# A four-stage transformer stack on one core: the instruction order of every engine chosen with another timing model

## The chip, the cores and the metric

The kernel runs on one core of one Trainium2 chip. The time is the device time of one execution in microseconds (us). The core's engines work side by side, each through its own list of instructions in a fixed order: TensorE (PE) multiplies matrices, VectorE (DVE) and ScalarE (ACT) do elementwise work, GpSimd (POOL) a little of it, and SyncE (SP) issues the transfers from memory. An instruction that has to wait holds up all that stand behind it on its engine. PE adds up its products in PSUM, a small memory from which DVE and ACT read them; everything else lies in SBUF.

## The reference

A sequence of 512 tokens of width 1024 goes through two blocks, all in float32. Only the shape of the work matters here:

```python
def first_block(x, mem, ...):
    h = token_mixer(rmsnorm(x, norm_mix_pre), ...)          # four kinds of token mixing, then @ w_mix_out
    x = x + rmsnorm(h, norm_mix_post)
    h = memory_cross_attention(rmsnorm(x, norm_cross_pre), rmsnorm(mem, mem_norm), wq, wk, wv, wo)
    x = x + rmsnorm(h, norm_cross_post)
    h = conv_glu_ffn(rmsnorm(x, norm_ffn_pre), w_up, conv_w, conv_b, w_down)
    x = x + rmsnorm(h, norm_ffn_post)
    return x

def second_block(x, ...):
    x = x + _even_mixer(x, ...)        # window attention and neighbourhood attention
    x = x + _mlp(x, norm, w1, w2)      # square(relu(h @ w1)) @ w2, hidden width 4096
    x = x + _odd_mixer(x, ...)         # retention with gates
    x = x + _mlp(x, norm, w1, w2)
    return x
```

What matters below are the three lines `x = x + rmsnorm(h, gain)` of the first block. The norm of a whole product `h` has to be known before anything of the next stage can start.

## The kernel before

The activations lie transposed: a row of the model width on each partition, the 512 tokens along the free axis, so the residual stream is eight tiles `X0` to `X7` of 128x512. Each float32 product is made of three faster ones. Both factors are split into a rounded high part and a low part (the rest), and `mm3` issues high by high (L272), high by low (L273) and low by high (L274). An activation is split by ACT (L280, high part, with the gain of the norm as scale) and DVE (L281, low part). A weight tile arrives by a transfer as `wf`, ACT casts it into `wh` (L315) and DVE takes the difference into `wl` (L316). There are four buffers for `wf`, six for `wh` and six for `wl`. A cast for a seventh tile therefore waits until PE has used the one six tiles back.

At the very start the norm of `x` is computed from eight squares (ACT) and sums (DVE L415), one product with a matrix of ones on PE (L420, `total`), then `rsqrt`: two ACT instructions (L295, L296) and three DVE instructions (L297 to L299). DVE L755 multiplies `X` by the result, and L280 and L281 split the product into the tiles `x` that the mixer's weights are multiplied with. While this runs, PE works on products with `mem`, for the cross attention.

The end of each of the mixer, the cross attention and the feed-forward part is written in `out_post`. I call the three places the boundaries. The tokens are worked on in two halves of 256, A and B:

1. The last output tiles are computed for half A, squared (ACT L414), summed (L415) and scaled by the gain (ACT L614). `norm(A)` then is L420 on PE, L295 and L296 on ACT, and L297 to L299 on DVE.
2. While PE computes half B of the last tiles, `update(A)` works through the eight tiles of the residual stream. For each there are four instructions: DVE L622 (times the norm), DVE L623 (add to `X`), ACT L280 and DVE L281 (split for the next stage's weights).
3. PE multiplies half A of the new `x` with three weight tiles of the next stage, 72 products of 128x256. The same is then done with half B, its squares being summed by POOL (L415) ahead of its norm. The squares of the new `X` (ACT L629, sums L631 and L633 on POOL or DVE) serve the norm of the next stage.

```python
def update(c, ms=range(NK)):
    for m in ms:
        x = self.X[m][:, c]
        nc.vector.tensor_tensor(hg[m][:, c], hg[m][:, c], r[:, c], op=ALU.mult)
        nc.vector.tensor_tensor(x, x, hg[m][:, c], op=ALU.add)
        self.split(xs[0][m][:, c], xs[1][m][:, c], x, scale=self.vec(nxt, m))
```

The order in which instructions stand on each engine isn't that of the program text. All is written inside a `TileContext`, which collects the instructions, their dependences and the buffers they need, and at its end lists them anew. It walks through time with a model of how long each instruction takes. Whenever an engine is free in the model, it appends the earliest instruction of the text whose inputs and buffers the model then takes to be ready. What the model thinks of durations and waits so decides which instruction comes first where several could. The order so found is fixed. On the chip each engine follows it, with semaphores for the dependences.

After the third boundary come the even mixer (to about 1060 us in the profiled execution), and then the first MLP, the odd mixer and the second MLP.

## Time and profile before

| | |
|---|---|
| time, median of 3 runs | 2175.26 us (2174.89 to 2177.64) |
| the profiled execution | 2179.55 us |
| its span (first to last instruction) | 2177.8 us |
| PE busy / weight loads / DVE / ACT / POOL | 98% / 83% / 72% / 53% / 2% |
| places where the stages end (boundaries) | 333 to 367, 404 to 444 and 786 to 821 us |

The profile is of one execution of the program. Each row gives instructions by the line of the kernel that issued them, their start and duration, and, where the engine stood idle before, for how long and what ended the wait. The profiled execution was 4.3 us longer than the median of the runs, and 1.75 us of it lie outside the span.

### The profile page before, as it was taken

The page shows a single profiled execution, that of the slowest core. Times are in us where ns is not written, and L with a number is a line of the kernel's source. Part 1 is how long each engine was busy: PE and PEld are TensorE (multiplying, and loading weights), DVE is VectorE, ACT ScalarE, POOL GpSimd, SP SyncE. Part 2 cuts the span into 40 slices and gives each one's busy share as a digit, 9 for nine tenths or more (in the row PEclk, how much of TensorE's full clock was granted, in tenths as well). Part 3 has the DMA queues.
Part 4 walks back from the last instruction along what each step waited for, and adds up shares of the span by engine and source line. Part 5 has one row for each costly group of instructions (what it writes and reads, how often), then busy time and mean ns, then how long its engine had stood idle before and what let it go on. Part 6 is the DMA issues. An engine that isn't in the chain of part 4 may idle for free.

```text
span 2177.8 us, 31728 instructions
## 1 busy us (share of the span) xinstructions
PE 2140.9 (98%) x11942; PEld 1813.0 (83%) x11942; DVE 1571.4 (72%) x2852; ACT 1153.9 (53%) x2124; POOL 34.5 (2%) x54
## 2 busy tenths in 40 slices
PE   8999998899999999999999999999999999999999
PEld 7877788788888897777889889888888888898997
DVE  8867758787774268887977586756776579875864
ACT  6555656665554246677645344555555456543542
POOL 0000001100000010000000000000000000000000
PEclk9999999999999999999999999999999999999999
DMA  5211241132233322221432331322222223323322
GB/s 172 70 64 63 77 142 59 49 102 95 95 96 91 92 71 93 66 73 39 141 101 94 97 107 59 104 88 73 69 72 88 68 95 129 107 96 97 105 72 68
DMA packets 94762, 192.68 MB, mean 88 GB/s; under 512 B 10512, under 2 KB 12176, under 8 KB 94608
## 3 DMA queue, kind: packets, MB, share of 16 engines
q1 hardware_dynamic: 93744, 189.01, 27.1%
q8 instruction: 93, 1.52, 0.3%
q10 hardware_dynamic: 864, 1.64, 0.2%
q14 instruction: 61, 0.50, 0.1%
HBM read 188.52 MB, written 2.10 MB: 88 GB/s over the span
## 4 chain that ended last, share of the span: by engine, by line
PE 89%; DVE 6%; ACT 2%; DMA 2%; issue 1%; SPq 0%; DVEq 0%; ACTq 0%
PE acc L272 19%; PE acc L273 19%; PE acc L274 19%; PE sc L272 6%; PE sc L273 5%; PE sc L274 5%; PE pt L274 2%; PE pt L272 2%; PE pt L273 2%; PE o L272 2%; PE o L274 2%; PE o L273 2%; PE pt L510 1%; PE sc L910 1%; PE pt L420 1%; DVE wl L316 1%
## 5 line engine op out<-in xcount | busy, mean ns | idle before, releaser
L315 ACT CAST wh<-wf 128x512 fp32r<-128x512 f32 (+1 forms) x548 | 334.1, 616 | 537.1 <-PE acc L273 429.6
L316 DVE TENSOR_TENSOR wl<-wf,wh 128x512 fp32r<-128x512 f32 (+1 forms) x548 | 368.5, 682 | 184.4 <-ACT wh L315 172.3
L272 PE MATMUL acc<-x,wh 128*128 128x512 f32 (+1 forms) x1104 | 427.7, 389 | 5.1 <-ACT x L280 3.2
L273 PE MATMUL acc<-x,wh 128*128 128x512 f32 (+1 forms) x1104 | 427.4, 388 | 1.2 <-DVE x L281 1.1
L274 PE MATMUL acc<-x,wl 128*128 128x512 f32 (+1 forms) x1104 | 426.1, 387 | 0.0
L272 PEld LDWEIGHTS acc<-x,wh 128*128 128x128 f32 x1104 | 209.9, 191 | 51.2 <-issue 3.7
L273 PEld LDWEIGHTS acc<-x,wh 128*128 128x128 f32 x1104 | 210.1, 190 | 45.5 <-issue 2.9
L274 PEld LDWEIGHTS acc<-x,wl 128*128 128x128 f32 x1104 | 210.2, 190 | 44.3 <-issue 2.2
L286 ACT CAST Wh<-F 128x1792 fp32r<-128x1792 f32 x64 | 108.2, 1693 | 101.0 <-PE pt L273 63.2
L287 DVE TENSOR_TENSOR Wl<-F,Wh 128x1792 fp32r<-128x1792 f32 x64 | 129.2, 2020 | 30.5 <-ACT Wh L286 30.1
L274 PE MATMUL acc<-y,wl 128*128 128x512 f32 x288 | 113.7, 395 | 0.0
L273 PE MATMUL acc<-y,wh 128*128 128x512 f32 x288 | 113.6, 395 | 0.0
L272 PE MATMUL acc<-y,wh 128*128 128x512 f32 x288 | 113.3, 393 | 0.0
L273 PE MATMUL sc<-x,wh 128*128 128x512 f32 (+1 forms) x264 | 97.9, 373 | 5.3 <-DVE x L281 5.2
L272 PE MATMUL acc<-wh,x 128*128 128x256 f32 (+1 forms) x352 | 98.8, 281 | 0.0
L274 PE MATMUL acc<-wh,x 128*128 128x256 f32 (+1 forms) x352 | 98.8, 281 | 0.0
L273 PE MATMUL acc<-wl,x 128*128 128x256 f32 (+1 forms) x352 | 98.8, 281 | 0.0
L274 PE MATMUL sc<-x,wl 128*128 128x512 f32 (+1 forms) x264 | 97.3, 370 | 1.3 <-DVE wl L316 1.3
L272 PE MATMUL sc<-x,wh 128*128 128x512 f32 (+1 forms) x264 | 96.7, 372 | 1.5 <-ACT x L280 1.1
L272 PE MATMUL acc<-h,wh 128*128 128x512 f32 (+1 forms) x220 | 74.2, 337 | 0.0
L274 PE MATMUL acc<-h,wl 128*128 128x512 f32 (+1 forms) x220 | 74.1, 337 | 0.0
L273 PE MATMUL acc<-h,wh 128*128 128x512 f32 (+1 forms) x220 | 74.1, 337 | 0.0
(517 smaller groups left out, 5162.1 us busy)
## 6 DMA issues: line engine op xcount, KB each, us to landing
F<-in_w_mlp_in_dram SPq DMA_DIRECT2D x64, 512.0 KB, 3.2
wf<-in_w_mlp_out_dram SPq DMA_DIRECT2D x128, 256.0 KB, 2.8
wf<-in_w_ffn_in_dram SPq DMA_DIRECT2D x88, 256.0 KB, 2.7
wf<-in_w_o_fm_dram SPq DMA_DIRECT2D x64, 256.0 KB, 2.7
wf<-in_w_in_fm_dram SPq DMA_DIRECT2D x44, 256.0 KB, 2.9
wf<-in_w_ffn_out_dram SPq DMA_DIRECT2D x40, 256.0 KB, 2.7
wf<-in_w_o_v_dram SPq DMA_DIRECT2D x32, 256.0 KB, 3.0
wf<-in_w_out_o_dram SPq DMA_DIRECT2D x32, 256.0 KB, 2.8
```

The costliest lines, as they stand in the source:

```text
L272: mm(ps, lhsT=lh, rhs=rh, start=start, stop=False, skip_group_check=True)
L273: mm(ps, lhsT=lh, rhs=rl, start=False, stop=False, skip_group_check=True)
L274: self.last_mm = mm(ps, lhsT=ll, rhs=rh, start=False, stop=stop, skip_group_check=True).ins
L286: nc.scalar.copy(hi, src)
L287: nc.vector.tensor_tensor(lo, src, self.f(hi), op=ALU.subtract)
L315: nc.scalar.copy(h[:, :n], wf[:, :n])
L316: nc.vector.tensor_tensor(l[:, :n], wf[:, :n], self.f(h[:, :n]), op=ALU.subtract)
L420: self.nc.tensor.matmul(ps[:, :n], lhsT=self.ones if mat is None else mat, rhs=acc[:, :n], start=True, stop=True)
L510: nc.tensor.transpose(pt[:, c:c + 128], P[:, at:at + 128], self.ident)
L910: mm = lambda out, pr, ss, ts: nc.tensor.matmul(out, lhsT=kq[0][pr, ss], rhs=kq[1][pr, ts], start=True, stop=True, skip_group_check=True)
```

## The change

The timing model that the `TileContext` orders instructions by is the timeline simulation instead of the default one. The instructions, the buffers and the dependences are the same; only their order on each engine differs.

```diff
--- before.py
+++ after.py
@@ -1745,7 +1745,7 @@
     out = nc.dram_tensor("out_0_dram", (D, T), F32, kind="ExternalOutput").ap()
-    with tile.TileContext(nc) as tc:
+    with tile.TileContext(nc, schedule_with_timeline_sim=True) as tc:
         build(tc, A, out)
```

Three places show what moved. In the rows `pt` is a norm's total, `s_6724` the half's norm at the third boundary, `s_6726` to `s_6733` the eight scaled tiles, `X_70` to `X_77` the residual stream, and `x_7795`, `x_7796` the high and low part of the first new tile.

PE, first norm at the start of the program, before:

```order
L272 MATMUL acc_107<-qk_95,wh_170 128x512
L273 MATMUL acc_107<-m_103,wh_170 128x512
L420 MATMUL pt_237<-s_106,ones 128x512
L274 MATMUL acc_107<-qk_95,wl_171 128x512
L272 MATMUL acc_108<-qk_95,wh_191 128x512
```

and now:

```order
L273 MATMUL acc_109<-m_103,wh_212 128x512
L274 MATMUL acc_109<-qk_95,wl_213 128x512
L272 MATMUL acc_109<-qk_96,wh_212 128x512
L420 MATMUL pt_237<-s_106,ones 128x512
L273 MATMUL acc_109<-m_104,wh_212 128x512
L274 MATMUL acc_109<-qk_96,wl_213 128x512
L274 MATMUL acc_108<-qk_97,wl_192 128x512
L272 MATMUL acc_109<-qk_97,wh_212 128x512
L273 MATMUL acc_109<-m_105,wh_212 128x512
L274 MATMUL acc_109<-qk_97,wl_213 128x512
L272 MATMUL sc_382<-wh_360,x_275 128x256
L273 MATMUL sc_382<-wl_361,x_275 128x256
```

The total (L420) stood 48th on PE and now stands 67th, so 19 products of 128x512 have come ahead of it. Between it and the first product that needs the norm (`sc_382`, 74th in both) six products are left.

ACT at the third boundary, before:

```order
L295 ACTIVATE s_6724<-pt_7715,eps 128x256
L296 ACTIVATE s_6724<-s_6724 128x256
L315 CAST wh_7817<-wf_7815 128x512
L315 CAST wh_7823<-wf_7821 128x512
L315 CAST wh_7829<-wf_7827 128x512
L280 ACTIVATE x_7795<-X_70,vecs 128x256
L629 ACTIVATE s_6726<-X_70 128x256
L280 ACTIVATE x_7797<-X_71,vecs 128x256
```

and now:

```order
L315 CAST wh_7817<-wf_7815 128x512
L315 CAST wh_7823<-wf_7821 128x512
L315 CAST wh_7829<-wf_7827 128x512
L295 ACTIVATE s_6724<-pt_7715,eps 128x256
L296 ACTIVATE s_6724<-s_6724 128x256
L315 CAST wh_7835<-wf_7833 128x512
L315 CAST wh_7841<-wf_7839 128x512
L414 ACTIVATE s_7875<-acc_7269 128x256
```

Three weight casts have moved ahead of the two ACT steps of `norm(A)`; on DVE their three L316 stand ahead of L297 to L299 in the same way. The first boundary has the same move with three casts. At the second one cast now stands ahead of L295 and one between L295 and L296, and the four L316 of its casts stand ahead of and between L297 to L299.

DVE at the third boundary from the end of `norm(A)` on, before:

```order
L299 SCALAR_TENSOR_TENSOR s_6724<-s_7717,s_6724 128x256
L622 TENSOR_TENSOR s_6726<-s_6726,s_6724 128x256
L622 TENSOR_TENSOR s_6727<-s_6727,s_6724 128x256
L316 TENSOR_TENSOR wl_7818<-wf_7815,wh_7817 128x512
L316 TENSOR_TENSOR wl_7824<-wf_7821,wh_7823 128x512
L316 TENSOR_TENSOR wl_7830<-wf_7827,wh_7829 128x512
L623 TENSOR_TENSOR X_70<-X_70,s_6726 128x256
L623 TENSOR_TENSOR X_71<-X_71,s_6727 128x256
L622 TENSOR_TENSOR s_6728<-s_6728,s_6724 128x256
L281 SCALAR_TENSOR_TENSOR x_7796<-X_70,vecs,x_7795 128x256
L623 TENSOR_TENSOR X_72<-X_72,s_6728 128x256
L281 SCALAR_TENSOR_TENSOR x_7798<-X_71,vecs,x_7797 128x256
```

and now, where eight L622 follow L299 ahead of these rows:

```order
L623 TENSOR_TENSOR X_70<-X_70,s_6726 128x256
L623 TENSOR_TENSOR X_71<-X_71,s_6727 128x256
L316 TENSOR_TENSOR wl_7836<-wf_7833,wh_7835 128x512
L623 TENSOR_TENSOR X_72<-X_72,s_6728 128x256
L316 TENSOR_TENSOR wl_7842<-wf_7839,wh_7841 128x512
L623 TENSOR_TENSOR X_73<-X_73,s_6729 128x256
L623 TENSOR_TENSOR X_74<-X_74,s_6730 128x256
L623 TENSOR_TENSOR X_75<-X_75,s_6731 128x256
L623 TENSOR_TENSOR X_76<-X_76,s_6732 128x256
L623 TENSOR_TENSOR X_77<-X_77,s_6733 128x256
L316 TENSOR_TENSOR wl_7848<-wf_7845,wh_7847 128x512
L281 SCALAR_TENSOR_TENSOR x_7796<-X_70,vecs,x_7795 128x256
```

The order was tile by tile: the first L281 stood ninth behind L299, with the tiles 4 to 8 still to be scaled. Now all eight L622, then all eight L623 and three L316 come first, and the first L281 is the twentieth behind L299. Half B is treated in the same way (eight L622, eight L623, then the L281), and so are both halves at the first boundary. At the second, half A is, and its last four L281 are mixed in among the L622 and L623 of half B.

## Rows read from the trace of the kernel before

**Rows 1.** The page: busy time, share of the span and instructions of each engine.

```profile
PE 2140.9 (98%) x11942; PEld 1813.0 (83%) x11942; DVE 1571.4 (72%) x2852; ACT 1153.9 (53%) x2124; POOL 34.5 (2%) x54
```

**Rows 2.** Stretches: us; PE, PEld, DVE, ACT, POOL busy; PE clock, DMA share, GB/s.

```profile
100.00:333.00 233.00, 229.56 (x1232) 177.35 (x1233) 156.54 (x351) 132.96 (x289) 4.87 (x16) 0.98 0.26 83
...
341.00:367.00 26.00, 21.47 (x153) 19.98 (x152) 24.44 (x54) 17.95 (x47) 7.35 (x10) 0.93 0.11 37
...
415.00:444.00 29.00, 23.70 (x145) 21.90 (x144) 26.41 (x55) 18.62 (x49) 10.05 (x12) 0.82 0.15 48
...
796.00:821.00 25.00, 21.52 (x150) 19.96 (x149) 25.00 (x53) 16.98 (x43) 10.34 (x10) 0.93 0.14 45
821.00:1100.00 279.00, 273.54 (x1452) 213.54 (x1451) 241.32 (x557) 186.25 (x395) 0.00 (x0) 1.00 0.25 82
1100.00:2178.00 1078.00, 1073.35 (x6156) 940.15 (x6154) 752.31 (x1168) 516.63 (x816) 0.00 (x0) 1.00 0.28 90
```

**Rows 3.** Timeline of PE at the start: start us, duration, instruction.

```profile
20.16 1.02 PE L420 MATMUL pt<-s,ones 128*128 128x512 f32 x2
...
21.25 0.39 PE L272 MATMUL acc<-qk,wh 128*128 128x512 f32 x1
...
26.57 0.40 PE L274 MATMUL acc<-qk,wl 128*128 128x512 f32 x1
26.80 0.28 PE L272 MATMUL sc<-wh,x 128*128 128x256 f32 x1
```

**Rows 4.** Timeline of ACT at the start.

```profile
25.91 0.72 ACT L280 ACTIVATE x<-s,vecs 128x512 fp32r<-128x512 f32 x1
```

**Rows 5.** Timeline of ACT at the third boundary.

```profile
788.96 0.47 ACT L295 ACTIVATE s<-pt,eps 128x256 f32<-128x256 f32 x1 [0.67 <-PE pt L420]
...
790.97 1.67 ACT L315 CAST wh<-wf 128x512 fp32r<-128x512 f32 x3 [1.09 <-PE acc L273]
```

**Rows 6.** Timeline of DVE at the third boundary.

```profile
791.30 0.76 DVE L622 TENSOR_TENSOR s<-s,s 128x256 f32<-128x256 f32 x2
791.97 1.89 DVE L316 TENSOR_TENSOR wl<-wf,wh 128x512 fp32r<-128x512 f32 x3
793.78 0.75 DVE L623 TENSOR_TENSOR X<-X,s 128x256 f32<-128x256 f32 x2
...
794.79 0.48 DVE L281 SCALAR_TENSOR_TENSOR x<-X,vecs,x 128x256 fp32r<-128x256 f32 x1
...
799.28 1.82 DVE L623 TENSOR_TENSOR X<-X,s 128x256 f32<-128x256 f32 x2
...
811.08 0.87 DVE L281 SCALAR_TENSOR_TENSOR x<-X,vecs,x 128x256 fp32r<-128x256 f32 x2
```

**Rows 7.** Timeline of POOL at the third boundary.

```profile
795.89 3.18 POOL L631 TENSOR_TENSOR acc<-s,s 128x256 f32<-128x256 f32 x1 [364.31 <-DMA wf<-in_w_e_a_dram]
799.03 2.65 POOL L415 TENSOR_TENSOR s<-s,s 128x256 f32<-128x256 f32 x3
```

**Rows 8.** Timeline of PE at the third boundary.

```profile
795.78 0.28 PE L272 MATMUL sc<-x,wh 128*128 128x256 f32 x1
...
801.74 0.70 PE L420 MATMUL pt<-s,ones 128*128 128x256 f32 x2 [1.24 <-POOL s L415]
...
811.14 0.45 PE L272 MATMUL acc<-x,wh 128*128 128x256 f32 x2
...
820.18 0.39 PE L272 MATMUL acc<-x,wh 128*128 128x512 f32 x1
```

**Rows 9.** Timeline of ACT at the first and the second boundary.

```profile
335.57 1.66 ACT L315 CAST wh<-wf 128x512 fp32r<-128x512 f32 x3 [1.07 <-PE acc L273]
...
409.19 0.47 ACT L295 ACTIVATE s<-pt,eps 128x256 f32<-128x256 f32 x1 [0.51 <-PE pt L420]
...
413.46 2.17 ACT L315 CAST wh<-wf 128x512 fp32r<-128x512 f32 x4
```

**Rows 10.** One stretch of half A at the third boundary, columns as in rows 2.

```profile
803.00:807.00 4.00, 3.71 (x18) 3.71 (x19) 4.00 (x10) 2.47 (x7) 1.55 (x3) 0.57 0.00 0
```

## What I expect of the change, and why

> **What bounds the kernel now.** I read the page first. PE is busy 98% of the span [rows 1]. Busy is not the same as working at full pace, so the second view is the table of stretches. It is to be read for two things: where PE was not busy, and which other engine was full there. From 1100 us to the end PE is busy 1073.35 of 1078 us while DVE is busy 752 [rows 2]. Nothing waits there, DVE and ACT run ahead of PE, and a new order costs and gives next to nothing. The early part is different. In the 26, 29 and 25 us of the three boundaries PE is busy only 21.47, 23.70 and 21.52 us, and DVE 24.44, 26.41 and 25.00 us [rows 2]. So at a boundary DVE sets the pace, and PE follows it. There the order in which DVE hands over tiles matters, and I went through these three places and the start instruction by instruction in the timeline.
>
> What a reader should see at the third boundary: the two halves, 72 products of the same shape each, start on PE at 795.78 and 811.14, and the next stage follows at 820.18 [rows 8]. Half B so takes 9.0 us, and half A took 15.4. Half A was slow because it kept step with DVE, which delivered one tile at a time from 794.79 on [rows 6]. The time was still used, since PE worked on each tile as it came.
>
> **The change part by part.** It adds and removes nothing, so all costs are waits.
>
> *The start.* PE issued the norm's total at 20.16 and the tile that needed it was split by ACT at 25.91 + 0.72 = 26.63 [rows 3, 4]. PE took it up at 26.80, with no wait. From 21.25 to 26.57 it did 23 products, 0.231 us each [rows 3]. Now 19 of these stand ahead of the total: 19 x 0.231 = 4.4 us later. The chain behind the total (ACT, DVE, ACT, 6.5 us) is as long as before, so the tile is ready at about 31.0. PE's own work ahead of it is the same and ends at 26.8. I take a wait of 4.2 us. The lower bound is 3, an allowance of about 1 us for the first products, which stand in another order too. The upper is 4.4. What covered this chain were the products now ahead of it; only six, 1.4 us, are left as cover. Nothing after it is late by itself; PE is simply 4 us behind.
>
> *The norm behind the casts.* At the third boundary ACT did L295 at 788.96, then waited 1.09 us for PE to free a weight buffer, and did three casts from 790.97 to 792.64 [rows 5]. Now the casts come first, and L295 starts at 792.64, 3.7 us later. Queued behind it on ACT are L296 and all of `update(A)`, on DVE L297 and everything after it. The first L622 came at 791.30, 2.34 us after L295 [rows 5, 6], and so now comes at about 795.0. The three L316, which came after it at 791.97 and took until 793.78, 1.8 us, now run ahead of it, so 1.9 of the 3.7 us are lost DVE time and 1.8 are moved work.
>
> *All tiles at once.* From 795.0 on DVE has eight L622 and eight L623 and three more L316 ahead of the first L281. L622 and L623 follow each other at 0.335 us (two L622 from 791.30 to 791.97 [rows 6]): 16 x 0.335 + 1.8 = 7.2 us, so the first L281 ends near 802.6. While POOL adds the three squares of half B (2.65 us [rows 7]), a DVE instruction took 0.91 instead of 0.335 us (two L623 in 1.82, 799.28 [rows 6]). That takes about 1.7 us more: 804.3. Until then PE can do two products of half A and the total of norm(B); in the kernel before the first L281 ended at 795.27. PE then works through half A without a wait, 9.0 us, to about 813.3, against 811.14 before. So half A costs only about 2 us, as it was slow before.
>
> Half B repeats it. From the first L281(A) on DVE has seven L281 at 0.4 us, three steps of norm(B) and sixteen L622 and L623 ahead of the first L281(B): 2.8 + 1.2 + 5.4 + 0.5 = 9.9 us, which gives 814.2. The POOL sums of the new squares, which slowed DVE before too, add 0 to 3.8 us; I take 2: 816. The second way of working it out gives more: 811.56 for the first L281(B) before (811.08 + 0.48 [rows 6]), 1.9 us of lost DVE time and some 12 L622 and L623 more ahead of it (4.1 us): 817.5. PE has then all 72 products still to do. 816 to 817.5 + 9.0 = 825.0 to 826.5, against 820.18: 4.8 to 6.3. I take 5. The lower bound is 1.3 (no POOL cost in either half, 812.5 + 9.0 = 821.5), the upper 6.5. At the first boundary the rows and the new order are alike (casts at 335.57 after a wait of 1.07 [rows 9]): 5, from 1.3 to 6.5. At the second the norm stood at 409.19 and four casts ended at 415.63 [rows 9]. L296 now waits for the second of them, and L299 for the fourth L316. That is later by 5 to 6 us instead of 3.7, but half B is mixed with half A and the low clock of the kernel before (0.82 [rows 2]) leaves PE slack. I take 5, from 2 to 8.
>
> *The mixer and the even mixer.* Here hundreds of instructions trade places, by up to 163 positions on DVE (weight splits L316 of the even output, brought forward ahead of attention steps). PE was idle 233 - 229.56 = 3.4 and 279 - 273.54 = 5.5 us there [rows 2]. A better order gains at most these 8.9 us; a worse one has no such limit, and I bound it by as much again, 8.9. The rows show no reason for a side, and I take 0.
>
> *The clock.* At the third boundary half A ran for about 3.4 of 4 us at the lower clock (0.57 granted from 803 to 807 [rows 10]) after PE had stood still several times. Four us at 0.57 is 1.7 us of work lost. I leave a new stretch of this kind at 0 in the sum, as the kernel before had them at all three boundaries, and carry up to 1.7 us for each of the four places in the range. [...]
>
> **The sum.** 4.2 + 5 + 5 + 5 + 0 = 19 us. The low ends give 3 + 1.3 + 1.3 + 2 - 8.9 = -1, the high ends 4.4 + 6.5 + 6.5 + 8 + 8.9 + 6.8 = 41. On the profiled execution (2179.55) this is 2198.7. That execution was 4.3 us above the median of the runs, with the same work, so for the median of the changed kernel I take 2175.3 + 19 = 2194.
>
> **The rivals.**
>
> *No change that can be measured* (within 0.2%, 4.4 us, about what a measurement of this kernel can tell from none). DVE is full at the boundaries before and after, its work is the same, and the last L281 of half B stands where it stood. If PE kept step with DVE to the end, only the 1.9 us of lost DVE time would count. Against it: the L281 of half B now come in one row, and PE needs 9 us from the first of them. With the casts no longer late (a buffer freed 1 us sooner) and half B taken in step, the boundaries would cost 1 us each, the start 3 and the mixers give 2: 2179.
>
> *Faster, through the second norm.* At the third boundary PE waited 1.24 us for POOL's sums of half B [rows 8], and all of half B hangs on them. POOL did the first sum of the new squares before them, 3.2 us [rows 7]; now half B's own squares come first, and norm(B) comes some 2 us sooner. If DVE then had half B's tiles ready before PE ends half A, half A's 15.4 us would shrink towards 9 and a boundary would gain 2 to 3 us. Three of them and half of the 8.9 us of the mixers, less 4.2 at the start: -8, 2167. It decides this way if the first L281(B) ends before PE has finished half A, at about 812; I work out 816. Against it speaks that DVE has no idle time there [rows 2].
>
> *Much slower, in the mixers.* In the even mixer DVE is busy 241 of 279 us [rows 2], more than anywhere else outside the boundaries. Some ten L316 and four low parts of x, 14 x 0.6 (the three L316 of [rows 6]) = 8 us of DVE work, now come ahead of attention steps on which PE waits. If PE runs dry there once or twice, the loss is not 0 but 10 to 20 us, with low clock behind each wait: 2210 to 2215.
>
> **How the numbers follow.** The forecast, 5 to 28 us slower, gets 0.64. Much slower, above 28 us, gets 0.14; no change 0.13; faster 0.09. Slower by over 0.2% is then 0.78. The range leaves out about 2 in 10: below it the faster rival and part of no change, above it the worse half of the mixers. It runs from 2178 (the low ends at the boundaries, with some gain in the mixers) to 2212.
>
> **What would show it.** At the start PE should stand idle for about 4 us ahead of the first product with `x`, released by ACT L280. At each boundary L295 should start right behind casts, the eight L622 and eight L623 should stand in a row, and PE should have one idle time of 6 to 9 us after two products of half A and a second one of 2 to 4 us ahead of half B, each released by DVE L281. From 1100 us on all should be as before but for a fixed shift. The forecast is wrong if half B starts without a wait at the boundaries, if PE's idle time in the mixers changes by more than 9 us, or if PE's pace itself changes.

## The result, and the profile after

The changed kernel takes 2277.78 us (median; 2272.19 to 2278.60), the kernel before 2175.36. The ratio of the runs is 1.0454, with an interval from 1.0441 to 1.0467. The medians are 102 us apart, and the ratio makes it some 99 us; below I go by the ratio. The forecast was 19 us, with 37 as the upper end. The profiled execution of the changed kernel took 2272.19 us, 5.6 less than its median, so what is read from it is a few us too small.

I cut both programs at five places where each engine has the same instructions behind it in both orders, and read how long each stage lasts on PE, from its first instruction to that of the next stage (the last to the end of PE's last product):

| stage | before | after | more | forecast |
|---|---|---|---|---|
| start | 75.7 | 84.9 | 9.2 | 4.2 |
| mixer | 212.3 | 238.3 | 26.0 | 0 |
| cross attention, with the first and second boundary | 311.9 | 320.3 | 8.4 | 10 |
| feed-forward rest, with the third boundary | 230.2 | 236.4 | 6.2 | 5 |
| even mixer | 242.1 | 281.4 | 39.2 | 0 |
| rest (both MLPs, odd mixer) | 1101.1 | 1104.6 | 3.5 | 0 |

The boundaries cost what the sum said. Of the 92 us that the stages add up to, seven tenths lie in the two stages for which the sum had 0. First the page of the changed kernel, the row that answers to [rows 1]:

```profile
PE 2180.2 (96%) x11942; PEld 1838.7 (81%) x11942; DVE 1572.5 (69%) x2852; ACT 1154.0 (51%) x2124; POOL 43.1 (2%) x54
```

DVE and ACT did the same work in the same time. PE was busy 39.3 us longer with the same instructions, and POOL 8.6 us longer. The stretches of the changed kernel, columns as in [rows 2]: the mixer, the three boundaries, the even mixer, the rest, and ten us at the start.

```profile
85.00:323.00 238.00, 226.10 (x1143) 170.19 (x1140) 168.80 (x377) 128.79 (x280) 6.55 (x16) 0.92 0.21 69
372.00:405.00 33.00, 24.26 (x168) 23.29 (x167) 28.44 (x68) 19.44 (x52) 12.60 (x10) 0.79 0.20 61
445.00:485.00 40.00, 29.25 (x208) 27.35 (x207) 34.78 (x75) 24.95 (x67) 10.18 (x12) 0.83 0.15 48
837.00:866.00 29.00, 19.04 (x130) 18.04 (x129) 25.46 (x61) 16.55 (x45) 12.57 (x10) 0.82 0.14 46
880.00:1161.00 281.00, 257.17 (x1196) 187.41 (x1194) 215.64 (x508) 166.52 (x364) 0.00 (x0) 0.94 0.19 62
1161.00:2270.00 1109.00, 1102.40 (x6370) 968.97 (x6370) 773.57 (x1202) 533.34 (x832) 0.00 (x0) 1.00 0.27 90
30.00:40.00 10.00, 6.77 (x26) 5.70 (x27) 10.00 (x17) 9.53 (x17) 0.00 (x0) 0.53 0.10 32
```

And the two mixers of the kernel before in the same cut:

```profile
76.00:288.00 212.00, 208.78 (x1142) 157.77 (x1141) 165.25 (x375) 127.20 (x277) 4.87 (x16) 0.98 0.23 75
830.00:1072.00 242.00, 237.76 (x1197) 180.02 (x1195) 209.64 (x506) 163.11 (x362) 0.00 (x0) 1.00 0.22 71
```

And its ten us at the start:

```profile
30.00:40.00 10.00, 9.99 (x79) 9.58 (x79) 10.00 (x17) 8.31 (x15) 0.00 (x0) 1.00 0.31 100
```

The even mixer shows how to read the pair of mixers. PE ran the same products (1196 and 1197 records). It was idle 281 - 257.17 = 23.8 us in place of 4.2, which is 19.6 us of waits. And PE was busy with the same products for 257.17 in place of 237.76 us, 19.4 more, at a granted clock of 0.94 in place of 1.00. In the mixer the idle time went from 3.2 to 11.9 us and the busy time from 208.78 to 226.10, at 0.92 in place of 0.98. Of the 65 us in both, 28 are so waits and 37 longer busy time. "PE is busy" hides the larger half.

The clock explains most of the 37 us and not all. By the rows, (1 - 0.92) x 238 + (1 - 0.94) x 281 = 36 us of clock were not granted in the two mixers, against (1 - 0.98) x 212 = 4 before, so it is at most 32. Part of that fell on idle time. Cut into 2076 stretches of 0.25 us, the two mixers of the changed kernel were granted 1.00 in 1777 of them and 0.50 in 276, with 23 between. PE was busy for 65 us at 0.50, against 10 before, and half of the difference is 27 us, an estimate from these two numbers. The other 10 of the 37 are not accounted for. Low clock and waits come together, but not in step. In the even mixer of e6 below PE was idle for 22.9 us at a clock of 0.97, in that of e2 for 20.6 us at 0.91. What brings the clock down in the mixers wasn't tried apart.

No single wait stands out. The waits of PE in the changed kernel (total us, times, longest):

```profile
PE pt L420 <- POOL s L415: 14.1, 3, 5.8
PE sc L272 <- ACT x L280: 12.6, 4, 4.2
PE acc L272 <- ACT wh L315: 6.4, 1, 6.4
PE pt L510 <- DVE Pl L287: 4.6, 7, 1.4
PE acc L272 <- ACT x L286: 4.5, 3, 2.0
```

The first two belong to the boundaries and the start, and the third was there before (6.2 us of it). In the mixers there are dozens of short ones, none over 2.0 us. So the question for the experiments was which engine's order makes them, and which instructions in it.

### The profile page after: what moved, and what is told of

Read it like the earlier page. It is cut to its first block, busy times and chain, and to the rows that moved or that the text cites. A ratio compares the mean times of both kernels' runs of the same rounds, so it can differ in the third digit from the quotient of the medians.

```text
span 2270.5 us, 31808 instructions
## 1 busy us (share of the span) xinstructions
PE 2180.2 (96%) x11942; PEld 1838.7 (81%) x11942; DVE 1572.5 (69%) x2852; ACT 1154.0 (51%) x2124; POOL 43.1 (2%) x54
## 4 chain that ended last, share of the span: by engine, by line
PE 78%; DVE 4%; ACT 3%; issue 1%; DMA 1%; POOL 0%; POOLq 0%; DVEq 0%; ACTq 0%; SPq 0%
PE acc L273 18%; PE acc L274 18%; PE acc L272 17%; PE sc L272 5%; PE sc L274 5%; PE sc L273 5%; PE pt L274 2%; PE pt L273 2%; PE pt L272 2%; PE o L272 1%; PE o L274 1%; PE o L273 1%; PE pt L420 1%; ACT P L495 1%; PE pt L510 1%
## 5 line engine op out<-in xcount | busy, mean ns | idle before, releaser
L316 DVE TENSOR_TENSOR wl<-wf,wh 128x512 fp32r<-128x512 f32 (+1 forms) x548 | 372.1, 684 | 252.8 <-ACT wh L315 227.1
L287 DVE TENSOR_TENSOR Wl<-F,Wh 128x1792 fp32r<-128x1792 f32 x64 | 129.4, 2022 | 43.5 <-ACT Wh L286 43.5
L286 ACT CAST Wh<-F 128x1792 fp32r<-128x1792 f32 x64 | 108.3, 1693 | 98.6 <-PE pt L273 54.4
```

Source lines behind the costliest of these rows:

```text
L286: nc.scalar.copy(hi, src)
L287: nc.vector.tensor_tensor(lo, src, self.f(hi), op=ALU.subtract)
L316: nc.vector.tensor_tensor(l[:, :n], wf[:, :n], self.f(h[:, :n]), op=ALU.subtract)
```

## The experiments

Each kernel is built with an order that is put together from the two. The program is listed once with each timing model, each engine's list is cut at the five places above, and for each stage and engine one of the two orders is imposed by dependences between neighbours, or none. Where none is, the scheduler orders that engine anew around the imposed ones, with the timeline model in the runs that start from the changed kernel and with the default model in those that start from the kernel before. POOL and SyncE are always left to it. The dependences set the place in the list. No wait added by them shows: in the even mixer of e1, with the lists of PE, DVE and ACT imposed, PE is busy for 237.23 of 242 us, in that of the kernel before for 237.76. In the program they are:

```diff
+            for names in chains:          # one list per engine, from the two orders
+                for a, b in zip(names, names[1:]):
+                    tc.add_manual_dep(traced[b], a, mybir.DependencyInfo(
+                        mybir.DependencyClass.NoSync, mybir.DependencyReason.DATA), reason="order")
```

"Above before" is the ratio less one, times 2175.4 us; stages in us on PE as above; "boundaries" are the third and fourth stage together. An interval reaches 3 to 5 us to either side, so a difference of less than some 5 us between two runs says nothing. In e2, e9, e12 and e13 the start is 1 to 3 us longer than in the changed kernel (86.2 to 87.4 in place of 84.9), as the mixer's first instruction waits there.

| run | median | ratio (interval) | above before | mixer | boundaries | even mixer |
|---|---|---|---|---|---|---|
| before | 2175.36 | 1 | 0 | 212.3 | 542.1 | 242.1 |
| after | 2277.78 | 1.0454 (1.0441 to 1.0467) | 98.8 | 238.3 | 556.7 | 281.4 |
| e1_mixers | 2201.93 | 1.0108 (1.0091 to 1.0126) | 23.5 | 210.7 | 555.1 | 242.0 |
| e4_ends | 2256.77 | 1.0363 (1.0345 to 1.0382) | 79.0 | 237.5 | 542.0 | 281.8 |
| e2_pe_only | 2251.80 | 1.0334 (1.0314 to 1.0355) | 72.7 | 223.0 | 554.6 | 280.6 |
| e3_dve_act | 2292.63 | 1.0525 (1.0506 to 1.0543) | 114.2 | 246.5 | 553.6 | 295.8 |
| e5_pe_alone | 2257.71 | 1.0372 (1.0354 to 1.0390) | 80.9 | 245.5 | 539.4 | 288.1 |
| e8_pe_dve | 2218.40 | 1.0188 (1.0170 to 1.0206) | 40.9 | 217.4 | 553.6 | 253.8 |
| e9_pe_act | 2238.89 | 1.0289 (1.0271 to 1.0307) | 62.9 | 215.8 | 556.1 | 270.3 |
| e6_products_held | 2251.42 | 1.0334 (1.0318 to 1.0350) | 72.7 | 233.1 | 553.6 | 268.7 |
| e7_products_first | 2241.09 | 1.0280 (1.0263 to 1.0297) | 60.9 | 238.7 | 541.1 | 279.0 |
| e12_splits_held | 2241.14 | 1.0285 (1.0270 to 1.0300) | 62.0 | 225.6 | 555.2 | 264.5 |
| e13_banks_first | 2225.48 | 1.0207 (1.0191 to 1.0224) | 45.0 | 216.5 | 553.7 | 253.8 |
| e10_norm_first | 2266.83 | 1.0417 (1.0398 to 1.0436) | 90.7 | 236.9 | 554.8 | 282.6 |
| e11_start | 2272.09 | 1.0426 (1.0411 to 1.0442) | 92.7 | 241.6 | 555.2 | 281.8 |
| e14_sums_dve | 2177.18 | 0.9989 (0.9980 to 0.9999) | -2.4 | 214.1 | 539.6 | 244.4 |

### Which stages: e1_mixers, e4_ends

The changed kernel with the old order put back in both mixers (e1), or from the first to the third boundary (e4).

```diff
-mixer, even: timeline order on PE, DVE, ACT
+mixer, even: default order on PE, DVE, ACT          (e1)
-cross, third: timeline order
+cross, third: default order                         (e4)
```

> The changed kernel, with the order of the kernel before on PE, DVE and ACT in two stages, the mixer and the even mixer; start, boundaries and all from the first MLP on keep the new order. By the traces these two stages took 26.0 and 39.2 us more. If the loss arises where the traces show it, the time falls by 62 to 68 us, to about 2213 us. If part of it was only handed on (late work that a stage behind it absorbs or that comes back as another wait), it falls by less than 50 us, and stays above 2228.

> The changed kernel with the order of the kernel before from the first boundary to the middle of the feed-forward part, and around the third boundary; start, mixer, even mixer and the rest are new. The traces give 8.4 us and 6.2 us for these stretches. If the boundaries' loss is their own, the time falls by 13 to 16 us, to about 2263 us. If it is only the lateness of the mixer that shows there, it falls by less than 8 us.

With the old order in the mixers 75 of the 99 us are gone (98.8 - 23.5), and with it at the boundaries 20. Both are more than was expected (62 to 68, and 13 to 16). The two make 95 and leave 4 for the start and the rest, which took 12.7 more by the stages; such sums are good to some 10 us. The even mixer of e1 is that of the kernel before, clock and all:

```profile
874.00:1116.00 242.00, 237.23 (x1275) 184.76 (x1273) 210.58 (x497) 166.77 (x358) 0.00 (x0) 1.00 0.22 74
```

So the mixers don't inherit anything from a late start or from the boundaries; the loss is made by the order inside them. Both numbers are larger than the stages of the profiled execution (65 and 15), by 10 and 5 us; that execution was 5.6 us shorter than its median.

### Which engine: e2_pe_only, e3_dve_act, e5_pe_alone, e8_pe_dve, e9_pe_act

All in the two mixers only. Four start from the changed kernel and put back the old order of one engine or two; the engines that aren't named in the cut are left to the timeline model. e5 goes the other way: the kernel before, with PE in the changed kernel's order and DVE and ACT left to the default model.

```diff
-mixer, even: timeline order on PE, DVE, ACT
+mixer, even: default order on PE                    (e2)
+mixer, even: default order on DVE, ACT              (e3)
+mixer, even: default order on PE, DVE               (e8)
+mixer, even: default order on PE, ACT               (e9)
 --- and from the kernel before
-mixer, even: default order on PE, DVE, ACT
+mixer, even: timeline order on PE, model's default for the rest   (e5)
```

> As the run with the old order in the mixer and the even mixer, but there only PE's order is that of the kernel before; DVE and ACT are ordered by the timeline model around it. Theory (cover): the new order takes the weight products, which need nothing but loaded weights, ahead of the attention steps, and leaves the attention chains at the end without products to run beside; then PE's order carries nearly all of the loss, and the time is 2210 to 2225 us. Rival (elementwise order): the weight splits brought forward on DVE delay the attention steps; then PE's order alone gives back little, and the time stays above 2250 us.

> The other half: in the mixer and the even mixer DVE and ACT have the order of the kernel before, and PE is ordered by the timeline model. PE's weight products then stand 28 and 32 places ahead of where they stood before on average (43 and 66 in the changed kernel). Cover theory: the loss shrinks about with these numbers, by a third in the mixer and by a half in the even mixer, 26 x 1/3 + 39 x 1/2 = 28 us: about 2250 us. Rival (elementwise order): the loss of the two stages is gone, about 2213 us.

> The kernel before (default timing model), with PE's order in the mixer and the even mixer taken from the changed kernel; DVE and ACT are ordered by the default model around it. PE's order alone, put back, gave 26 us. If PE's order is bad by itself (weight products used up early), it costs here what it costs in the changed kernel, 40 us or more: 2215 to 2245 us. If the loss lies in how the timeline model orders DVE and ACT, the default model makes up for most of it, and the time is below 2195 us.

> The changed kernel, with PE and DVE in the order of before in the mixer and the even mixer, and ACT ordered by the timeline model. With PE's order alone put back the time was 2252 us, with PE, DVE and ACT 2202 us. PE's waits in the first of these runs were mostly for low parts made by DVE. Theory: DVE's order carries the remaining 50 us, and the time is 2200 to 2212 us. Rival (ACT's order, on which the high parts and the exponentials depend): it stays above 2235 us.

> The counterpart: PE and ACT in the order of before in the mixer and the even mixer, DVE ordered by the timeline model. If DVE's order carries the remaining 50 us, the time stays at 2235 to 2255 us. If ACT's order does, it falls to 2200 to 2212 us. If both have to fit together with PE, both this run and its counterpart stay well above 2212.

How these runs read depends on where the engines that were left to the model ended up. In e2 DVE and ACT did not keep the changed kernel's order. Over the two mixers a DVE instruction of e2 stands 4 places from its place in the kernel before, in the mean, and 11 from that in the changed kernel; on ACT it is 1 and 9. In e5 it is the reverse: around PE's new order the default model put DVE and ACT within 2.5 and 1 places of the changed kernel's order. So e5, 81 us slower than the kernel before and nearly the whole loss, is the changed kernel's mixers built again from the other side: PE's order brings the rest with it. And e2 gives back only 26 of the 99 us, 1 of them in the even mixer (280.6 against 281.4), because the model then finds another bad order for DVE and ACT, near the old one.

Three runs differ from e1 in the mixers on one engine alone, since the other two have the old order in both:

| run | what differs from e1 | mean distance from the old place | us above e1 |
|---|---|---|---|
| e3 | PE | 32 places | 91 |
| e9 | DVE | 3 places | 39 |
| e8 | ACT | 0.6 places | 17 |

PE's order does harm with DVE and ACT exactly as before. In e3 it isn't the changed kernel's either: weight products stand 28 and 32 places ahead of the old order, in place of 43 and 66, and yet the run is 15 us slower than the changed kernel. But small moves on DVE and ACT cost tens of us too, and the number of places says little on the price. How the 75 us of the change divide among the engines isn't shown: no run has PE's old order beside the changed kernel's order on DVE and ACT, or the other way round.

Of what was expected, e9 came out (DVE). e2 came out on its rival's side (above 2250 us), by 2 us, e5 above its range by 13, e8 by 6, and e3 above both of its theories. A list of one engine can't be judged without those of the others.

### Which instructions on PE: e6_products_held, e7_products_first

The mixers' work on PE is of two kinds. Weight products (`acc<-x,wh`, `wl`) need only loaded weights and can run at any time. Attention steps wait for a chain: scores (`sc`) go to ACT and DVE, which make `P`; PE transposes `P` (L510, `pt`); ACT and DVE split the transposes into `Ph` (L286) and `Pl` (L287); PE multiplies these with `v` (`o`). The timeline model brings weight products forward, by 43 places in the mean in the mixer and 66 in the even mixer, and attention steps fall back by 56 and 51. The longest row of PE instructions without a weight product grows from 45 to 130 in the mixer and from 67 to 111 in the even mixer. e6 forbids that: in the changed kernel no weight product may come ahead of an attention step that it followed before. e7 does nothing but that: in the kernel before, attention steps have to stand behind the weight products that they follow in the new order.

```diff
+# e6, from the changed kernel
+for x in PE_order["before"][stage]:
+    if x not in weight_products: last = x
+    elif last: chains.append([last, x])
+# e7, from the kernel before
+for x in PE_order["after"][stage]:
+    if x in weight_products: last = x
+    elif last: chains.append([last, x])
```

> The changed kernel; in the mixer and the even mixer one rule only is added to the timeline model's order: on PE no weight product may stand ahead of an attention step that it followed in the kernel before. All else there, on PE, DVE and ACT, is the model's choice. With PE's whole order put back the time was 2252 us. If what is bad in PE's order is that weight products come early, the time is 2245 to 2262 us here too. If it is the order of the attention steps among themselves, it stays above 2270 us.

> The kernel before (default model) with the opposite rule: in the two mixers an attention step on PE may not stand ahead of a weight product that it follows in the changed kernel. The default model chooses all else. With PE's whole order of the changed kernel this made 2258 us. If early weight products are the cause, the time is 2235 to 2260 us. If the order among the attention steps is, it is below 2200 us.

Both came out in their ranges. e7 costs 61 of the 81 us of e5, and its lists stand within 1 to 3 places of the changed kernel's on PE, DVE and ACT: one rule on PE is enough to build most of the changed order and of the loss. So on PE it is the weight products that came early. e6 gives back 26 us, as e2 does, but not in the same place (5 us in the mixer and 13 in the even mixer, where e2 gives 15 and 1), so that the totals agree is chance. Like e2, it leaves DVE and ACT to the timeline model, and what it gives back is no measure of what the early products cost. The trace shows what they do. The timeline of PE in the even mixer of the changed kernel (start, duration, instruction, and in brackets the idle time before it and who ended it):

```profile
973.32 0.44 PE L510 MATMUL pt<-cm,P 128*128 128x128 f32 x2 [1.12 <-DVE Pl L287]
...
975.68 0.33 PE L272 MATMUL o<-Ph,v 128*64 128x256 f32 x1 [0.42 <-ACT Ph L286]
...
978.83 0.44 PE L510 MATMUL pt<-cm,P 128*128 128x128 f32 x2 [1.38 <-DVE Pl L287]
979.29 3.56 PE L420 MATMUL pt<-s,cm 128*128 128x512 f32 x4
984.04 1.13 PE L420 MATMUL pt<-s,cm 128*128 128x512 f32 x2 [1.18 <-DVE s L298]
986.63 1.12 PE L1339 MATMUL pt<-cm,s 128*128 128x128 f32 x4 [1.47 <-DVE s L298]
989.13 0.69 PE L510 MATMUL pt<-cm,P 128*128 128x128 f32 x2 [1.39 <-DVE s L298]
```

and the same kind of work in the kernel before:

```profile
1016.11 0.39 PE L273 MATMUL acc<-x,wh 128*128 128x512 f32 x1
1016.34 0.49 PE L510 MATMUL pt<-cm,P 128*128 128x128 f32 x3
1016.59 0.42 PE L272 MATMUL o<-Ph,v 128*64 128x384 f32 x1
1016.85 0.40 PE L274 MATMUL acc<-x,wl 128*128 128x512 f32 x1
1017.08 0.38 PE L510 MATMUL pt<-cm,P 128*128 128x128 f32 x2
```

Before, weight products, 0.23 us apart, stand between the links of the chain, and PE doesn't wait there. After, from 968 to 1001 us there isn't one, and PE has ten waits of 0.15 to 1.5 us. From 986.5 to 990 us the granted clock is 0.50, and the same instructions take longer there: two L510 0.69 us (989.13) in place of 0.44 at 1.00 (973.32 and 978.83), four L1339 1.12 us (986.63) in place of 0.60 at 1.00 in the kernel before, at 1010.84. The stretch in the middle of it:

```profile
970.00:990.00 20.00, 12.51 (x47) 5.91 (x45) 15.07 (x38) 12.46 (x27) 0.00 (x0) 0.82 0.00 1
```

The last two columns, 0.00 and 1 GB/s, say that next to no transfer ran. The last weight difference ahead of the stretch, and the first weight product behind it:

```profile
965.01 0.69 DVE L316 TENSOR_TENSOR wl<-wf,wh 128x512 fp32r<-128x512 f32 x1 [1.04 <-ACT wh L315]
```

```profile
1001.83 0.50 PE L272 MATMUL acc<-x,wh 128*128 128x512 f32 x1
```

No weight tile is cast or split between 965.70 and 1003 us, and PE starts these products without a wait. The weights that could have covered the waits were there all the time; their products stood behind the attention steps in PE's list.

### Which instructions on DVE: e12_splits_held, e13_banks_first

Both start from e2 (PE's old order in the mixers). They explain what is left there, and the changed kernel only by analogy, as its DVE order is another. In e12 a weight difference (L316) may not come ahead of a DVE instruction that it followed before; the rival of the prediction named these. In e13 nothing may come ahead of a low part `Pl` that it followed before. The transposes have two `pt` banks in PSUM, and a bank is free only when `Pl` has been taken. In e2 the L316 stand 3 places ahead of their old place in the mixer and 12 in the even mixer, and `Pl` 1.9 and 4.5 places later. In the changed kernel it is 30 and 42 places, and 10.4 and 12.3.

```diff
+# e12: held = weight differences;  e13: held = all but the low parts Pl
+for x in DVE_order["before"][stage]:
+    if x not in held: last = x
+    elif last: chains.append([last, x])
```

> The changed kernel with PE's order of before in the two mixers, as in the run of 2252 us, and one rule on DVE: no weight difference (L316) may stand ahead of an attention step that it followed in the kernel before. With DVE's whole order of before the time was 2218 us. If the weight differences brought forward are what is bad in DVE's order, as the rival on record said, it falls to 2215 to 2230 us. If it is the order among the attention steps on DVE, it stays above 2243 us.

> The changed kernel with PE's order of before in the two mixers (2252 us so far) and one rule on DVE: nothing may stand ahead of a low part of the attention weights (L287 into Pl, which frees the transposes' PSUM bank) that it followed in the kernel before. PE waited most for these in the 2252 us run, and the link from the scaled weights to the transposes is 13.1 us there against 7.5. If the late freeing of banks is what is bad in DVE's order, the time falls to 2212 to 2228 us, near the 2218 of DVE's whole old order. If it is something else on DVE, it stays above 2238 us (with the weight differences held back alone it was 2241).

e12 gives 10.7 us and lies between its two ranges, e13 gives 27.7, as expected. Together that is a little more than DVE's whole share (e2 to e8: 31.8), so they seem to overlap. The waits of PE in e2 that hang on it, and then what is left in e13:

```profile
PE pt L510 <- DVE Pl L287: 11.0, 10, 2.4
...
PE sc L272 <- ACT qk L286: 4.9, 3, 2.6
```

```profile
PE sc L272 <- ACT qk L286: 2.3, 3, 1.4
```

The 11 us of waits for a bank are down to 1.9 or less in e13, and the stages gain more than that, 33 us (e2 to e13, both mixers). In the changed kernel these waits came to 4.6 us (the list further up). The even mixer of e2 and of e13:

```profile
865.00:1146.00 281.00, 260.38 (x1199) 194.49 (x1199) 214.46 (x510) 166.72 (x364) 0.00 (x0) 0.91 0.19 64
```

```profile
872.00:1126.00 254.00, 242.21 (x1256) 185.76 (x1256) 211.51 (x503) 166.65 (x359) 0.00 (x0) 0.99 0.22 70
```

Idle time falls by 8.8 us (20.6 to 11.8) and busy time by 18.2, with the granted clock back from 0.91 to 0.99.

One measure goes with the even mixer's length over most runs: the mean time of a head from its first score product to its last value product (16 heads, worked out from the timeline). It is 31.0 us in before and e1 (stage 242), 32.2 in e13 (254), 34.0 in e12 (265), 35.7 in after (281), 37.0 in e2 (281) and 37.4 in e5 (288). 16 heads times that, over the stage, is close to two heads in flight in each of them. That the stage is long because each head is, at two heads in flight, is argued from this; the number of heads in flight was not changed in any run.

### The boundaries and the start: e10_norm_first, e11_start, e14_sums_dve

e10 is the changed kernel with the norm of half A ahead of the casts again, at all three boundaries: its total, L295 and L296, and L297 to L299. e11 is the changed kernel with the first total 48th on PE again, L295 and L296 ahead of the cast and L297 to L299 ahead of the difference that had passed them. e14 is the kernel before with the boundary sums that POOL does given to DVE.

```diff
-L315 x3 .. L295 L296        (ACT; DVE alike: L316 x3 .. L297 L298 L299)
+L295 L296 .. L315 x3        (e10, three boundaries)
-PE: total 67th
+PE: total 48th, L295 to L299 ahead of the cast and difference   (e11)
 --- and from the kernel before
-        evac([(m, *t) for m, t in zip(split, tail)], nc.gpsimd)
+        evac([(m, *t) for m, t in zip(split, tail)], nc.vector)
-        squares(A, nc.gpsimd)
+        squares(A, nc.vector)                                   (e14)
```

> The changed kernel, with one thing put back at the three boundaries: the total of norm(A) on PE, L295 and L296 on ACT and L297 to L299 on DVE stand ahead of the weight casts and their differences again. All eight tiles at once stays. The prediction's working gave 1.9 us of lost DVE time per boundary to the norm behind the casts and the rest to the tiles at once; the new trace has norm(A) 2.6 us late at the third boundary. By that the time falls by 5 to 8 us. If only the tiles at once matter, it falls by less than 3; if only the late norm matters, by 13 to 16.

> The changed kernel with the first norm put back at the start: the total on PE behind 47 products instead of 66, L295 and L296 on ACT ahead of the casts of the tenth and later weight tiles, L297 to L299 on DVE ahead of their differences. The tiles all at once (eight L755 and L763 ahead of the first L281) stay. The start took 9.2 us more by the traces. If the total's lateness of 4.2 us and the low clock behind the wait are the cause, the time falls by 5 to 9 us, to about 2271 us. If the tiles all at once decide, it falls by less than 3 us.

> The kernel before (default model), with the sums that POOL does at the boundaries (L415 of half B, L631 and L633 of half A) done by DVE. While POOL worked, a DVE instruction took 0.91 instead of 0.335 us, and POOL did ten such sums per boundary. If each sum on POOL holds DVE up by more than the 0.335 us that DVE needs for it, the three boundaries gain 2 us each: 2167 to 2173 us. If DVE and POOL only share the time, the boundaries get longer by the added DVE work, 3 us each, and the time is 2177 to 2185 us.

*e10* gives 8 us by the ratio, the upper end of what was expected, but the two boundary stages are only 1.9 us shorter in its profile, so most of the 8 isn't shown to lie there. The casts ahead of the norm are at most a part of the boundaries' 15 to 20 us. What is left is the row of tiles, and what it does to POOL. The third boundary of the changed kernel, on DVE, on POOL and on PE:

```profile
837.38 2.77 DVE L622 TENSOR_TENSOR s<-s,s 128x256 f32<-128x256 f32 x8
...
844.56 2.67 DVE L281 SCALAR_TENSOR_TENSOR x<-X,vecs,x 128x256 fp32r<-128x256 f32 x3
849.47 1.06 DVE L281 SCALAR_TENSOR_TENSOR x<-X,vecs,x 128x256 fp32r<-128x256 f32 x1 [2.24 <-ACT x L280]
```

```profile
839.70 5.52 POOL L415 TENSOR_TENSOR s<-s,s 128x256 f32<-128x256 f32 x1 [368.31 <-ACT s L414]
...
845.29 1.65 POOL L415 TENSOR_TENSOR s<-s,s 128x256 f32<-128x256 f32 x2
```

```profile
842.17 0.50 PE L272 MATMUL sc<-x,wh 128*128 128x256 f32 x2 [3.26 <-ACT x L280]
847.00 1.22 PE L420 MATMUL pt<-s,ones 128*128 128x256 f32 x2 [4.33 <-POOL s L415]
...
857.92 0.51 PE L272 MATMUL acc<-x,wh 128*128 128x256 f32 x2 [0.68 <-ACT x L280]
860.12 0.58 PE L273 MATMUL acc<-x,wh 128*128 128x256 f32 x1 [1.70 <-DVE x L281]
```

POOL's three sums of half B took 7.25 us in place of 2.65 [rows 7], and the first of them 5.52. While it lasted, DVE kept its 0.335 us for each L622 and L623. The sum ended after DVE had come to its first L281 (844.56), and from there the two took turns: three L281 in 2.67 us and two sums in 1.65. The first boundary shows the same, with 5.57 us for the first sum. In the kernel before, too, a POOL sum (L631, 3.18 us [rows 7]) lasted through a row of L622 and L316 on DVE until an L281 came, and in the turns behind it an L623 took 0.91 us [rows 6].

The total of norm(B) stands third in half A on PE, so all of half A waited 4.33 us for POOL. At the three boundaries that is 14.1 us (the waits above). At the second, with 5.8 of them, POOL's five sums took 4.44 us, 0.89 each as in [rows 7], but began late. No run has the changed kernel with these sums on DVE, so what the hold-up costs it isn't shown.

So in three rows of L622, L623 and L316 a POOL sum that ran beside the row took 3.18, 5.52 and 5.57 us, where each of the three L415 in [rows 7] took 0.88, and it ended only when DVE had come to an L281. Why it ended there isn't shown.

*e14* takes POOL out of it in the kernel before. DVE takes over the sums at 0.42 us:

```profile
800.52 0.42 DVE L415 TENSOR_TENSOR s<-s,s 128x256 f32<-128x256 f32 x1
```

It comes out at 0.9989, 2.4 us, at the edge of what can be measured and between the two ranges that were expected. The cross and third stages are 2.5 us shorter. POOL's help is worth about as much as what it slows in the old order; it isn't clearly a better kernel.

*e11* gives 6 us by the ratio, as expected, and the start itself only 1.9 us (83.0 against 84.9). The other 4 aren't found in its profile, which is no shorter than that of the changed kernel (2272.56 against 2272.19 us). In the changed kernel, PE and DVE at the start:

```profile
30.12 0.39 PE L272 MATMUL sc<-wh,x 128*128 128x256 f32 x1 [4.18 <-ACT x L280]
...
34.83 0.58 PE L274 MATMUL sc<-wh,x 128*128 128x256 f32 x1 [2.26 <-DVE x L281]
```

```profile
28.62 2.50 DVE L755 TENSOR_TENSOR s<-X,rstd 128x512 f32<-128x512 f32 x4
31.04 1.88 DVE L763 TENSOR_TENSOR m<-acc,rstd 128x512 f32<-128x512 f32 x3
32.83 1.28 DVE L755 TENSOR_TENSOR s<-X,rstd 128x512 f32<-128x512 f32 x2
34.03 2.73 DVE L281 SCALAR_TENSOR_TENSOR x<-s,vecs,x 128x512 fp32r<-128x512 f32 x4
```

With the total back at 19.72 in e11 (23.52 in the changed kernel), the norm ended 4 us earlier, but DVE took the first L755 at 27.68, only 0.9 us earlier:

```profile
23.72 0.69 DVE L299 SCALAR_TENSOR_TENSOR rstd<-s,rstd 128x512 f32<-128x512 f32 x1
24.33 0.69 DVE L316 TENSOR_TENSOR wl<-wf,wh 128x512 fp32r<-128x512 f32 x1
26.03 0.69 DVE L316 TENSOR_TENSOR wl<-wf,wh 128x512 fp32r<-128x512 f32 x1 [1.01 <-issue]
27.07 0.69 DVE L316 TENSOR_TENSOR wl<-wf,wh 128x512 fp32r<-128x512 f32 x1 [0.35 <-ACT wh L315]
27.68 2.49 DVE L755 TENSOR_TENSOR s<-X,rstd 128x512 f32<-128x512 f32 x4
```

Three weight differences stand between, and the second and third start late, the third for its cast. PE's first wait only falls to 2.56 us, and the second, for L281 behind six L755 and three L763, stays (2.41). The late total was one of two causes in a row, and the second was hidden behind it.

## Why the prediction was wrong

The sign was right, and the size was not: 99 us, where the range ended at 37.

*The step that failed* is "The mixer and the even mixer": "The rows show no reason for a side, and I take 0", with 8.9 us at either end. The rows gave a bound on a gain, the idle time of PE. I mirrored it as the bound on a loss, with no reason but symmetry, a sentence after saying that a loss has no such limit. What it measured is 65 us by the stages and 75 by e1, and the prediction's own signs of being wrong were there: PE's idle time in the mixers grew by 28 us, where 9 was the limit, and its pace changed. The reason for a side was there to be read before any run, in PE's list: weight products forward, attention steps back, rows of over a hundred PE instructions without a weight product. I had looked at DVE's list there (its largest move is 136 places, not 163; on PE it is 197), and at the boundaries, where the engines wait. PE had next to no waits in the mixers *because* weight products lay between the links of the chains; e7, which only brings them forward, makes the waits (23.2 us of idle time in 279 us of the even mixer, 830 to 1109, against 4.2). What covers a chain shows up in a trace as the absence of waits, and so I took it for free. The list gives the side of the loss but not its size: e3 moves the products less far and loses more.

*The rival "much slower, in the mixers"* had the right place, and with 10 to 20 us too small a loss. Its mechanism, L316 ahead of attention steps on DVE, has no price for the changed kernel. From e2, where the L316 stand less far ahead, holding them back gives 10.7 us (e12). PE's own order (e3, e5, e7) and the low parts `Pl` that free the transposes' banks (e13, from e2) were not in it.

*The clock* was carried as up to 1.7 us at each of four places. In the mixers, where the sum had none, it cost 27 to 32 us at 0.92 and 0.94. Over the whole span the clock not granted, (1 - 0.972) x 2270.5 = 64 us against (1 - 0.993) x 2177.8 = 15, grew by 48 us, and PE's idle time by 53. The term was right in kind, too small by a factor of four or more against the 6.8 us of the four places, and left out of the two stages where most of it lay.

*The start* was put at 4.2 us and took 9.2. The wait for ACT L280 came out as worked out (4.18), with some luck: the first split tile and the end of PE's work ahead of it (25.94 in place of 26.8) both came about 0.9 us earlier than told. Missed were 2.26 us for L281, as six L755 and three L763 now stand ahead of the first one, and 0.85 for L763. I had worked through "all tiles at once" at the boundaries and not at the start, where the same model makes the same move. The clock was the third thing missed: 0.53 was granted from 30 to 40 us, behind the wait of 4.18 us, where the kernel before was granted 1.00. The sum had 0 for that, and only the range had its 1.7 us.

*The boundaries* were put at 15 and took 14.6 by the stages, 20 by e4. That is right in size and partly by luck. The eight L622 and L623 stand in a row, and at the third boundary PE waits at half A and again at half B, as told. The lengths fit too, 3.26 + 4.33 = 7.6 us (6 to 9 were told) and 0.68 + 1.70 = 2.4 us (2 to 4). But of these only the last is ended by DVE L281. The first ends with ACT L280, and the largest with POOL's sums. I had POOL slow DVE down (1.7 us), as in the kernel before; it was POOL that was held up first, and PE that waited for it.

*From 1100 us on* all was as before but for 3.5 us, as told (1102.40 of 1109 us busy).

*The rivals "faster" and "no change"* fall with e4: at the boundaries the old order is 20 us better, and no norm that came sooner made up for it.

## What to carry to other kernels

When a scheduler's model changes, look on the busiest engine for the instructions that could run at any time, and ask what they covered. That gives the side of the loss. Its size can't be read from the list: neither the places moved nor the longest row without such an instruction followed it here (in the even mixer that row is 67 in e2, 72 in e3 and 111 in the changed kernel, and the stage takes 281, 296 and 281 us). A stage with no idle time bounds what a better order can gain and says nothing on what a worse one can lose, so its range has to be wide on that side. When one engine's order is put back and the others are left to a scheduler, compare their lists too before the difference is called that engine's. Judge PE by its busy time for the same products as well as by its waits, since here more of the loss lay there.

## What the runs showed of the hardware

Two things I had not expected. While DVE worked through a row of L622, L623 and L316 (128x256 and 128x512), at 0.335 us for each L622 and L623, one 128x256 sum on POOL took 5.5 us, at two boundaries. It ended when DVE came to an L281, and from there the two took turns, with 0.8 us for a sum and about 0.9 for a DVE instruction. And in the two mixers, where the waits are many and none is over 2.0 us, the granted clock over the whole stage was 0.92 and 0.94 in place of 0.98 and 1.00; the busy time of the same products grew by more (37 us, 27 to 32 of them by the clock) than the waits did (28).
